# Two attention heads at a time: float32r scores over stacked rows, and forget sums added in masks by GpSimd

## The chip, the cores and the metric

The kernel runs on one core of one Trainium2 chip. The metric is device time in microseconds (us) of one execution. The engines of the core are PE (TensorE, matrix multiplication), ACT (ScalarE), DVE (VectorE), POOL (GpSimd) and SP (SyncE, which here only starts transfers). Each engine takes its own instructions in the order in which they are written, and waits on semaphores for the others.

## The reference, cut to what matters

Two layers of a decoder trunk are computed for 256 tokens of width 1024. Each layer is a half-step FFN, a mixer and a second half-step FFN. The change lies in the mixer. It has three groups of attention heads that read one projection `P = rms_norm(h) @ w_in`:

```python
# A: 4 heads that share one key and value head; each query keeps its top 64 keys
s = jnp.einsum('bqhd,bqkd->bhqk', qb, kg) * scale        # only selected keys
# B: 4 heads, causal; with 256 tokens one block, so plain causal attention
# C: 8 heads with a forget gate
log_f = log_sigmoid(cf + forget_bias)
c = cumsum(log_f, axis=1)                                # per head, over tokens
s = einsum(q, k) * scale + c[query] - c[key]             # then causal mask, softmax
o_c = (softmax(s) @ v) * sigmoid(cg)
h = h + concat(o_a, o_b, o_c) @ w_out
```

In C, queries and keys are RMS-normed per head of 64 values. All of it is float32.

## The kernel before, in words

Weights are streamed from HBM by SP in pieces of 1 MB into five buffers (`raw`). Each piece is split into a high part `wh` (ACT rounds it to float32r, line 117) and a low part `wl` (DVE subtracts, line 121). This splitting is called from many places as `W.pump()`. A float32 product is made as three float32r products (high x high, high x low, low x high; `mm3`).

The order of all work is the order in which the Python code emits it (`manual_schedule`): there is no scheduler. Tiles come from rotating pools, so an instruction can also wait until the last reader of a buffer is done. The PSUM tag `gu` has four banks, and so has `acc`.

A mixer is first a projection in eight chunks of four steps, 32 steps in all (`iq, ib, b, a, ck, cq, cv, cg`). Beside the matmuls of each step run the side jobs registered by `at_step(n, job)`: rotary embedding and norms on POOL, the indexer and its top-k on DVE, the whole of the four B heads, and at step 29 (`SUMS_STEP`) the cumulative forget sums `c` by a matmul with a triangle of ones.

Then comes the stage that the change rewrites, here called the A/C stage: the four A heads, the eight C heads, and between their pieces, as filler for PE, ten half-steps of the output projection (`out_halves`: six matmuls of 512 columns each, from `oT`, the transposed outputs of head pairs that are ready). It ends in `tail`, which does the rest of the output projection and begins the next norm. One head is five jobs:

- `scores(i)`: PE multiplies queries by keys into a `gu` bank; DVE adds a mask, takes the row maximum and writes to SBUF (line 1024, one instruction for each of two query blocks). A heads use float32r in two products (keys split into high and low). C heads use one float32 product of 66 rows (`cT`): 64 values, and two rows that carry `c` and ones, so that the product adds `c[query] - c[key]`. The mask of C is the plain causal one.
- `exps(i)`: two exponentials on ACT (lines 1031, 1032).
- `flip(i)`: three PE transposes into a bank, copied to SBUF by DVE (even heads) or ACT (odd heads) (line 1040).
- `values(i)`: PE multiplies with the values; DVE divides by the sum (lines 1054, 1060, 1063).
- `outT(j)`: for a pair of heads, two PE transposes, then ACT rounds to the high part (line 1078) and DVE subtracts for the low part (line 1079).

`c_T(j)` transposes queries and keys of a pair of C heads, eight PE transposes of 66 columns, one copy each on ACT and DVE (lines 1137, 1138). The loop runs over single heads: scores of head i, flip of head i-1, exponentials of head i, a `c_T`, an output half, an `outT`, values of head i-1.

Of the kernel before, what the change touches and what calls it, by code (L numbers as in the profile page):

```python
# [18 lines left out]
P = 128  # L19
S = 256  # L20
# [15 lines left out]
DOWN_LAG = 4  # L36
OUT_TAIL = 3
WARM = 6
BRIDGE = 3
# [102 lines left out]
def kernel(ctx: ExitStack, tc: tile.TileContext, x, ffn1_norm, ffn1_w_gate, ffn1_w_up, ffn1_w_down,  # L142
# [148 lines left out]
    identr = cp.tile([P, P], F32R, name="identr")  # L291
    cqa = [at.tile([P, 8, 66], F32, name=f"cqa{t}", tag=f"cqa{t}") for t in range(2)]
    cka = [at.tile([P, 8, 66], F32, name=f"cka{t}", tag=f"cka{t}") for t in range(2)]
    va = [at.tile([P, 13, 65], F32, name=f"va{t}", tag=f"va{t}") for t in range(2)]
    for t in range(2):
        G.memset(cqa[t][:, :, 65:66], 1.0)
        G.memset(cka[t][:, :, 64:65], 1.0)
        G.memset(va[t][:, :, 64:65], 1.0)
# [311 lines left out]
    def tail(acc, rhs, ks, factor, make_norm, late=None):  # L610

        nxt = make_norm()
        ws = dict(zip(ks, [W.take() for _ in ks]))

        def part(q, some):
            for k in some:
                tokens(acc[q], q, rhs[k], ws[k], False, k == ks[-1])

        ahead = [0] * 4
        if late:
            part(0, ks[:1])
            late[0]()
            part(0, ks[1:2])
            part(1, ks[:1])
            late[1]()
# [33 lines left out]
    def mixer(l, norm, nxt):  # L661
# [109 lines left out]
        def post_ib(ps):  # L771
# [182 lines left out]

        c_ss = at.tile([P, 2, 2, 8], F32, name="c_ss", tag="c_ss")

        def c_sums(i, dst, ps, when):
            sq = []
            for t in range(2):
                evac(dst[t][:, :, 0:64], heads(ps[t], 8), t)  # L960
                sq.append(squares(ps[t], t, 8))
# [7 lines left out]
        def post_ck(ps):  # L969
            c_sums(0, cka, ps, 21)  # L970

        def post_cq(ps):
            c_sums(1, cqa, ps, 25)
            for t in range(2):
                q = cqa[t][:, :, 0:64]
                G.tensor_tensor(q, q, gc[:, None, :].to_broadcast([P, 8, HD]), op=ALU.mult)

            def c_norm():
                rs = head_rs(c_ss.rearrange("p i t h -> p (i t h)"), 32, "c")
                for t in range(2):  # L980
                    for i, d in enumerate((cka, cqa)):
                        x = d[t][:, :, 0:64]
                        scale_heads(x, x, rs[:, 16 * i + 8 * t:16 * i + 8 * t + 8])

            at_step(25, c_norm)

        def post_cv(ps):
# [14 lines left out]
        def run_heads(hs, qk, tag, emit=None):  # L1002
            pj, pt, op = {}, {}, {}

            def scores(i):

                kind, h = hs[i]
                q, k = qk(kind, h)
                b = bank(tag)
                if kind == "C":  # L1010
                    mm(b[:, 0:P], q[:, 0:P], k[:, 0:P], True, True)
                    mm(b[:, P:3 * P], q[:, P:S], k[:, 0:S], False, True)
                else:
                    products(b[:, 0:P], q[:, 0:P], [c[:, 0:P] for c in k], True, True)
                    products(b[:, P:3 * P], q[:, P:S], [c[:, 0:S] for c in k], False, True)
                mask = st["amask"] if kind == "A" else causal
                s = tmp(3 * P)
                nm = sm.tile([P, 2], F32, name="nm", tag="nm")
                for t, c in enumerate((slice(0, P), slice(P, 3 * P))):
                    scale = -1.0  # L1020
                    if kind != "C":
                        col = (5 * t if kind == "A" else 4 * t) + h
                        scale = st["r" + kind.lower()][:, col:col + 1]
                    V.tensor_tensor_reduce(s[:, c], b[:, c], mask[:, c], scale, 3e38, op0=ALU.add, op1=ALU.min,
                                           accum_out=nm[:, t:t + 1])
# [39 lines left out]
            def outT(i):  # L1065
# [12 lines left out]
                A.copy(hh, b[:, :S])  # L1078
                V.tensor_tensor(hl, b[:, :S], hh.bitcast(F32), op=ALU.subtract)
                oT[k] = (hh, hl)  # L1080

            if emit is None:
                return scores, exps, flip, values, outT
            for fn, whens in ((scores, (-0.5, 0.5, 1.5, 2.5)), (exps, (0.25, 1.25, 3.25, 3.5)),
                              (flip, (2.6, 2.7, 4.6, 4.7)), (values, (4.3, 4.4, 5.3, 5.4)), (outT, (8.3, 8.4))):
                for i, when in enumerate(whens):
                    emit(when, lambda fn=fn, i=i: fn(i))

# [39 lines left out]

        c_both = xp.tile([P, 2, 8, S], F32, name="cT", tag="xhl")
        cT = [c_both[:, 0], c_both[:, 1]]  # L1130

        def c_T(hp_):
            for d, src in zip(cT, (cqa, cka)):
                b = bank("gu")
                for i in range(2):
                    for t in range(2):
                        T.transpose(b[:66, i * S + t * P:i * S + (t + 1) * P], src[t][:, 2 * hp_ + i, :], ident)  # L1137
                (A.copy if src is cqa else V.tensor_copy)(d[:66, 2 * hp_:2 * hp_ + 2],
                                                         b[:66].rearrange("p (a b) -> p a b", a=2))

        def qk_ac(kind, h):
            if kind == "A":
                return st["aqT"][:, h], [st["akT"][:, c, 0] for c in range(2)]
            return cT[0][:66, h], cT[1][:66, h]
# [3 lines left out]
        n = len(hs)  # L1148
        next(halves)
        for i in range(n + 1):  # L1150
            if i < n:
                scores(i)
            if i > 0:
                flip(i - 1)
            if i < n:
                exps(i)
            if i in (1, 3, 5, 7):
                c_T(i // 2)
            if i not in (3, 5, 7, n):
# [7 lines left out]
        return tail(acc, oT, OUT_ORDER[8 - OUT_TAIL:], 1.0, nxt,  # L1167
                    (lambda: values(n - 1), lambda: outT(n // 2 - 1)))

# [59 lines left out]
```

## Time and profile before

| what | value |
|---|---|
| median of 3 runs | 1038.47 us (1037.96 to 1039.38) |
| profiled execution | 1038.33 us |
| its span in the profile | 1036.6 us |
| busy share PE, DVE, ACT, POOL | 100%, 78%, 57%, 14% |
| granted TensorE clock | 1.0 of full speed |

The span is what the profile covers, from the first to the last instruction of the core; the time of the execution has some 1.7 us around it. Busy shares are averages over the whole program. A matmul's record includes its way through the array, so consecutive records overlap, and short waits of PE do not show in its busy share; starts of successive instructions, or the chain of work, tell what a matmul costs in a row. In the layer that is looked at, the projection ends and the A/C stage begins at 289.5 us of the span, and the next FFN begins at 336.8 us. The second layer runs the same code.

### The profile page before, as it was taken

What the parts mean: (1) busy time and instruction counts of PE and PEld (TensorE: products, weight loads), DVE (VectorE), ACT (ScalarE), POOL (GpSimd) and SP (SyncE); (2) the same over time, 40 slices, a digit from 0 to 9 for tenths busy, and PEclk for the clock granted to TensorE, in tenths of its full rate; (3) what the DMA queues carried; (4) which work ended last, traced back from release to release, by engine and by line L of the source; (5) the groups of instructions that cost most, each with busy time, mean ns of one, the idle gap of its engine ahead of it and who ended that gap; (6) DMA issues with size and microseconds to landing.
All of it is one profiled execution on the core that took longest, in us unless ns stands there. A gap on an engine that the chain in (4) does not pass through costs nothing.

```text
span 1036.6 us, 15084 instructions
## 1 busy us (share of the span) xinstructions
PE 1032.3 (100%) x5641; PEld 898.8 (87%) x5641; DVE 808.9 (78%) x1537; ACT 591.8 (57%) x1045; POOL 148.2 (14%) x177
## 2 busy tenths in 40 slices
PE   9999999999999999999999999999999999999998
PEld 8888888898888888888888888888988988888887
DVE  6978778789876877777788777787898768777776
ACT  6655555666854655555465555557676546555552
POOL 2003000167800000000000110002766000000000
PEclk9999999999999999999999999999999999999999
DMA  9674656555431364645645564664555224554631
GB/s 320 222 244 157 214 185 198 182 190 174 154 131 42 123 230 144 236 163 206 200 163 195 180 219 150 241 185 174 163 194 172 83 67 159 182 199 167 232 134 40
DMA packets 130808, 181.61 MB, mean 175 GB/s; under 512 B 7040, under 2 KB 104624, under 8 KB 130736
## 3 DMA queue, kind: packets, MB, share of 16 engines
q1 hardware_dynamic: 130704, 180.66, 51.5%
q8 instruction: 44, 0.72, 0.3%
q14 instruction: 28, 0.23, 0.1%
q10 hardware_dynamic: 32, 0.01, 0.0%
HBM read 179.60 MB, written 1.05 MB: 174 GB/s over the span
## 4 chain that ended last, share of the span: by engine, by line
PE 99%; DMA 1%; SPq 0%; DVE 0%; issue 0%
PE ps_gu L302 66%; PE ps_acc L302 30%; PE ps_acc L337 1%; PE ps_gu L1038 1%; PE ps_gu L1137 1%; DMA trunk<-in_x_dram 1%; PE ps_acc L739 0%; PE ps_acc L1038 0%; PE ps_gu L1071 0%; PE ps_acc L494 0%; SPq L91 0%; PE ps_acc L363 0%; PE ps_acc L1071 0%; SPq L190 0%; DVE trunk L376 0%
## 5 line engine op out<-in xcount | busy, mean ns | idle before, releaser
L121 DVE TENSOR_TENSOR wl<-raw,wh 128x1024 fp32r<-128x1024 f32 (+2 forms) x342 | 416.9, 1225 | 24.9 <-ACT wh L117 24.9
L117 ACT CAST wh<-raw 128x1024 fp32r<-128x1024 f32 (+2 forms) x341 | 343.0, 1036 | 5.7 <-PE ps_gu L302 4.9
L302 PE MATMUL ps_gu<-xhl,wh 128*128 128x512 f32 x1408 | 330.4, 390 | 0.0
L302 PEld LDWEIGHTS ps_gu<-xhl,wh 128*128 128x128 f32 x1408 | 262.7, 188 | 53.9 <-ACT wh L117 0.4
L302 PEld LDWEIGHTS ps_gu<-xhl,wl 128*128 128x128 f32 x1408 | 176.1, 191 | 4.2 <-issue 0.2
L302 PE MATMUL ps_gu<-xhl,wl 128*128 128x256 f32 x1408 | 179.1, 283 | 0.0
L302 PE MATMUL ps_gu<-wh,xhl 128*128 128x512 f32 (+2 forms) x512 | 157.2, 377 | 0.0
L441 DVE TENSOR_TENSOR tmp<-ps_gu,tmp 128x256 f32<-128x256 f32 x176 | 72.9, 422 | 107.7 <-ACT tmp L440 107.4
L302 PE MATMUL ps_acc<-wh,hh 128*128 128x512 f32 (+1 forms) x352 | 137.2, 390 | 0.0
L302 PE MATMUL ps_acc<-wl,hh 128*128 128x512 f32 (+1 forms) x352 | 137.0, 389 | 0.0
L302 PE MATMUL ps_acc<-wh,hl 128*128 128x512 f32 (+1 forms) x352 | 136.5, 388 | 0.0
L440 ACT COPY tmp<-ps_gu 128x256 f32<-128x256 f32 x176 | 63.5, 371 | 93.3 <-PE ps_gu L302 93.1
L302 PEld LDWEIGHTS ps_gu<-wh,xhl 128*128 128x128 f32 x512 | 94.8, 188 | 14.6
L455 ACT CAST hh<-tmp 128x256 fp32r<-128x256 f32 x80 | 32.6, 407 | 120.0 <-DVE tmp L452 120.0
L302 PE MATMUL ps_gu<-wl,xhl 128*128 128x512 f32 (+2 forms) x256 | 95.7, 374 | 0.0
L447 ACT ACTIVATE tmp<-tmp 128x256 f32<-128x256 f32 x88 | 36.9, 419 | 81.9 <-DVE tmp L445 81.6
L313 POOL TENSOR_TENSOR y_n<-msq,minus_half 128x2 f32<-128x2 f32 x6 | 6.8, 1141 | 529.7 <-DVE msq L312 529.7
L302 PEld LDWEIGHTS ps_acc<-wh,hl 128*128 128x128 f32 x352 | 66.1, 188 | 13.9
L302 PEld LDWEIGHTS ps_acc<-wh,hh 128*128 128x128 f32 x352 | 66.2, 188 | 12.6
L302 PEld LDWEIGHTS ps_acc<-wl,hh 128*128 128x128 f32 x352 | 66.3, 188 | 12.2
L302 PEld LDWEIGHTS ps_gu<-wl,xhl 128*128 128x128 f32 x256 | 48.2, 188 | 6.7
L326 ACT ACTIVATE xhl<-ps_acc,gT 128x256 fp32r<-128x256 f32 x48 | 19.1, 474 | 39.2 <-PE ps_acc L337 35.7
(221 smaller groups left out, 1010.8 us busy)
## 6 DMA issues: line engine op xcount, KB each, us to landing
raw<-in_ffn_w_down_dram SPq DMA_DIRECT2D x44, 1024.0 KB, 4.9
raw<-in_ffn_w_gate_dram SPq DMA_DIRECT2D x42, 1024.0 KB, 6.6
raw<-in_ffn_w_up_dram SPq DMA_DIRECT2D x42, 1024.0 KB, 7.5
raw<-in_w_in_dram SPq DMA_DIRECT2D x24, 1024.0 KB, 4.9
raw<-in_w_out_dram SPq DMA_DIRECT2D x8, 1024.0 KB, 4.9
raw<-in_w_in_dram SPq DMA_DIRECT2D x4, 768.0 KB, 4.9
raw<-in_w_in_dram SPq DMA_DIRECT2D x4, 656.0 KB, 4.0
raw<-in_ffn_w_gate_dram SPq DMA_DIRECT2D x3, 512.0 KB, 7.1
```

Of the source, the lines that this page charges most:

```text
L117: self.nc.scalar.copy(hv, src)
L121: (engine or self.nc.vector).tensor_tensor(lv, self.srcs[self.n_low], hv.bitcast(F32), op=ALU.subtract)
L302: T.matmul(o, l, r, start=start, stop=stop, skip_group_check=True)
L313: G.tensor_tensor(y, dst, minus_half[:, :n], op=ALU.pow)
L326: A.activation(self.h[:, m], src, AF.Copy, scale=gT[:, self.col + m:self.col + m + 1])
L337: T.transpose(ps[:, i, t * P:(t + 1) * P], trunk[:, t, (2 * mp + i) * P:(2 * mp + i + 1) * P], ident)
L440: A.copy(o, ps[:, 1])
L441: V.tensor_tensor(o, ps[:, 0], o, op=ALU.add)
L447: A.activation(th, t_, AF.Tanh, scale=0.5)
L455: (V.tensor_copy if late else A.copy)(hh, t_)
L1038: T.transpose(b[:, j * P:(j + 1) * P], pj[i][:, j * P:(j + 1) * P], ident)
L1137: T.transpose(b[:66, i * S + t * P:i * S + (t + 1) * P], src[t][:, 2 * hp_ + i, :], ident)
```

## The change

The A/C stage takes two heads at a time. The C scores no longer carry the forget sums in two extra rows. Queries and keys are now 128 stacked rows of float32r: the query's high part over its low part, and the key twice; the key's high and low parts are two products, as in A. The forget sums go into the mask: `c` is transposed by PE at step 30, its negative is written by ACT to a row buffer in DRAM and, at step 31, read back by one transfer that repeats it on all 128 partitions (8 heads x 256 values, 1 MB in SBUF). POOL then makes the masks for two heads at once, in place (`decay`), and prepares the stacked queries and keys (`c_parts`). The scaling of keys by their norm moves from `c_norm` to `c_parts`. In `c_T` both copies are now on ACT and a subtraction on DVE follows. `outT` gives back its DVE part, to be emitted between the two scores of the next pair. `HALVES` says how many output halves stand in each of the six iterations; two stand ahead of the loop.

```diff
+HALVES = (1, 2, 1, 1, 2, 1)
...
+dram = ctx.enter_context(tc.tile_pool(name="dram", bufs=1, space=bass.MemoryType.DRAM))
...
-                for t in range(2):
-                    c = b[:, 8 * t:8 * t + 8]
-                    A.copy(cqa[t][:, :, 64], c)
-                    A.activation(cka[t][:, :, 65], c, AF.Copy, scale=-1.0)
+                st["c"] = sm.tile([P, 2, 8], F32, name="c", tag="c", bufs=1)
+                A.copy(st["c"].rearrange("p t h -> p (t h)"), b[:, 0:16])
+
+            def turn_sums():
+                b = bank("acc")
+                for t in range(2):
+                    T.transpose(b[:8, t * P:(t + 1) * P], st["c"][:, t], ident)
+                n = tmp(S)[:8]
+                A.activation(n, b[:8, :S], AF.Copy, scale=-1.0)
+                st["row"] = dram.tile([8, S], F32, name="minus_c_row", tag="minus_c_row")
+                nc.scalar.dma_start(st["row"], n)
+
+            def load_sums():
+                d = st["row"]
+                st["minus_c"] = at.tile([P, 8, S], F32, name="minus_c", tag="kT")
+                nc.scalar.dma_start(st["minus_c"], bass.AP(tensor=d.tensor, offset=d.offset,
+                                                           ap=[[0, P], [S, 8], [1, S]]))
 
             at_step(SUMS_STEP, cumsum)
+            at_step(SUMS_STEP + 1, turn_sums)
+            at_step(SUMS_STEP + 2, load_sums)
...
+        def c_parts(j):
+            hs2 = slice(2 * j, 2 * j + 2)
+            q = tp.tile([P, 512], F32R, name="stacked", tag="tmp")
+            q4 = q.rearrange("p (t h s d) -> p t h s d", t=2, h=2, s=2)
+            A.copy(q4[:, :, :, 0], cq[:, :, hs2])
+            G.tensor_tensor(q4[:, :, :, 1], cq[:, :, hs2], q4[:, :, :, 0].bitcast(F32), op=ALU.subtract)
+            k = tmp(512)
+            k4 = k.rearrange("p (t h s d) -> p t h s d", t=2, h=2, s=2)
+            for t in range(2):
+                G.tensor_tensor(k4[:, t], ck[:, t, hs2, None, :].to_broadcast([P, 2, 2, HD]),
...
+        def decay(j):
+            m = st["minus_c"][:, 2 * j:2 * j + 2]
+            c = st["c"][:, :, 2 * j:2 * j + 2, None]
+            first = at.tile([P, 2, P], F32, name="first", tag="first", bufs=2)
+            tri2 = causal[:, None, 0:P].to_broadcast([P, 2, P])
+            G.tensor_tensor(first, m[:, :, 0:P], c[:, 0].to_broadcast([P, 2, P]), op=ALU.add)
+            G.tensor_tensor(first, first, tri2, op=ALU.add)
+            G.tensor_tensor(m, m, c[:, 1].to_broadcast([P, 2, S]), op=ALU.add)
+            G.tensor_tensor(m[:, :, P:S], m[:, :, P:S], tri2, op=ALU.add)
...
+            at_step(31, lambda: c_parts(0))
...
-                    mm(b[:, 0:P], q[:, 0:P], k[:, 0:P], True, True)
-                    mm(b[:, P:3 * P], q[:, P:S], k[:, 0:S], False, True)
+                    masks = decays.pop(h)
...
+            for i in range(2):
+                for t in range(2):
+                    mm(bq[:, i * S + t * P:i * S + (t + 1) * P], q[:, t, i], identr, i + t == 0, True)
+            for i in range(2):
+                for t in range(2):
+                    T.transpose(bk[:, i * S + t * P:i * S + (t + 1) * P], k[:, t, i], ident)
...
+            A.copy(d[:, 0], bq)
+            A.copy(d[:, 1], bk)
+            V.tensor_tensor(d[:, 2], bk, d[:, 1].bitcast(F32), op=ALU.subtract)
...
+        two(0, scores)
+        c_parts(1)
+        decay(0)
+        two(0, exps)
         next(halves)
...
+        next(halves)
+        for k in range(n):
+            last = k == n - 1
+            two(k, flip)
+            low = outT(k - 1) if k else None
+            if not last:
+                scores(2 * k + 2)
+            if low:
+                low()
+            if not last:
+                scores(2 * k + 3)
+                two(k + 1, exps)
+            if k < 4:
+                c_T(k)
+            if k < 3:
+                if k < 2:
+                    c_parts(k + 2)
+                decay(k + 1)
+            if not last:
+                two(k, values)
+            for _ in range(HALVES[k]):
                 next(halves)
-            if 0 < i < n:
-                if i > 2 and i % 2:
-                    outT((i - 3) // 2)
-                values(i - 1)
+            if last:
+                two(k, values)
```

More of the change, by code (lines that the diff above doesn't have):

```diff
@@ L622, in tail @@
         if late:
-            part(0, ks[:1])
-            late[0]()
-            part(0, ks[1:2])
+            part(0, ks[:2])
             part(1, ks[:1])
-            late[1]()
+            late()
             part(1, ks[1:2])
@@ L1009, in scores @@
                 b = bank(tag)
+                products(b[:, 0:P], q[:, 0:P], [c[:, 0:P] for c in k], True, True)
+                products(b[:, P:3 * P], q[:, P:S], [c[:, 0:S] for c in k], False, True)
                 if kind == "C":
[L1011 to L1016 removed]
+                    masks = decays.pop(h)
+                else:
+                    m = st["amask"] if kind == "A" else causal
+                    masks = m[:, 0:P], m[:, P:3 * P]
                 s = tmp(3 * P)
@@ L1078, in outT, with low @@
                 A.copy(hh, b[:, :S])
[L1079 removed]
                 oT[k] = (hh, hl)
+                def low():
+                    V.tensor_tensor(hl, b[:, :S], hh.bitcast(F32), op=ALU.subtract)
+                return low
             if emit is None:
@@ L1143, in qk_ac, with two @@
                 return st["aqT"][:, h], [st["akT"][:, c, 0] for c in range(2)]
-            return cT[0][:66, h], cT[1][:66, h]
+            d = cT[:, h // 2 % 2]
+            return d[:, 0, h % 2], [d[:, 1, h % 2], d[:, 2, h % 2]]
         hs = [("A", h) for h in range(4)] + [("C", h) for h in range(8)]
         scores, exps, flip, values, outT = run_heads(hs, qk_ac, "gu")
-        n = len(hs)
-        next(halves)
[L1150 to L1159, printed above, removed]
+        n = len(hs) // 2
+        def two(k, *fns):
+            for fn in fns:
+                fn(2 * k)
+                fn(2 * k + 1)
+        two(0, scores)
+        c_parts(1)
+        decay(0)
+        two(0, exps)
+        next(halves)
+        next(halves)
[19 more added lines that the diff above has]
+            for _ in range(HALVES[k]):
                 next(halves)
-            if 0 < i < n:
-                if i > 2 and i % 2:
-                    outT((i - 3) // 2)
-                values(i - 1)
+            if last:
+                two(k, values)
         for _ in halves:
             raise AssertionError
-        return tail(acc, oT, OUT_ORDER[8 - OUT_TAIL:], 1.0, nxt,
-                    (lambda: values(n - 1), lambda: outT(n // 2 - 1)))
+        return tail(acc, oT, OUT_ORDER[8 - OUT_TAIL:], 1.0, nxt, lambda: outT(n - 1)())
     def before_mixer(l):
```

44 lines of the change are left out of this document (22 added, 22 removed).

## The prediction

> **What bounds the kernel now.** I read the page first, then the A/C stage: its busy times, the chain of work and the instructions in order of time.
>
> ```profile
> span 1036.6 us, 15084 instructions
> ...
> PE 1032.3 (100%) x5641; PEld 898.8 (87%) x5641; DVE 808.9 (78%) x1537; ACT 591.8 (57%) x1045; POOL 148.2 (14%) x177
> ...
> PE 99%; DMA 1%; SPq 0%; DVE 0%; issue 0%
> ```
>
> PE is the chain from end to end. The stage that is rewritten, and in it the order of work on PE (start, duration, what):
>
> ```profile
> core 0: us, PE busy (x) PEld busy (x) DVE busy (x) ACT busy (x) POOL busy (x), PEclk, DMA share, GB/s
> 289.50:336.90 47.40, 47.40 (x306) 41.82 (x306) 32.77 (x112) 24.09 (x54) 0.00 (x0) 1.00 0.21 70
> ```
>
> ```profile
> 292.91 0.46 PE ps_gu L302 x4
> ...
> 310.44 1.32 PE ps_gu L302 x10
> 311.76 0.33 PE ps_gu L1038 x3
> 312.09 0.87 PE ps_gu L1137 x8
> 312.96 0.22 PE ps_gu L1071 x2
> ...
> 314.89 1.39 PE ps_acc L302 x6
> ```
>
> The granted clock is full (1.00) and PE goes from piece to piece without a gap; DVE is at 32.77 of 47.40 us (69%), ACT at 51%, POOL does nothing. So the stage is worth what its PE instructions cost, as long as the others keep up. A flip takes 0.33 us of PE, a c_T 0.87, an outT 0.22, an output half 1.39, values and scores of a C head together 1.32, scores of an A head alone 0.46. How the others follow, as instructions of one C head:
>
> ```profile
> 296.38 0.71 PE L302 MATMUL ps_gu<-akT,aqT 128*128 128x128 f32 x4
> 297.13 0.35 DVE L1024 CUSTOM_DVE_ANT_0 tmp<-ps_gu,amask,minus_a 128x128 f32<-128x128 f32 x1
> ...
> 310.27 0.78 PE L302 MATMUL ps_gu<-va,pT 128*128 128x65 f32 x6
> 310.89 0.87 PE L302 MATMUL ps_gu<-cT 66*128 66x128 f32 x4
> 311.09 0.17 DVE L1054 RECIPROCAL ri<-ps_gu 128x2 f32<-128x2 f32 x1 [0.47 <-PE ps_gu L302]
> ...
> 311.80 0.29 DVE L1024 CUSTOM_DVE_ANT_0 tmp<-ps_gu,causal 128x128 f32<-128x128 f32 x1
> ...
> 312.36 0.55 DVE L1040 COPY pT<-ps_gu 128x384 f32<-128x384 f32 x1
> 312.50 0.49 ACT L1032 ACTIVATE p<-tmp,nm 128x256 f32<-128x256 f32 x1
> 312.90 0.56 ACT L1138 COPY cT<-ps_gu 66x512 f32<-66x512 f32 x1
> 313.37 0.36 ACT L1078 CAST oh<-ps_gu 128x256 fp32r<-128x256 f32 x1
> 313.76 0.42 DVE L1079 TENSOR_TENSOR ol<-ps_gu,oh 128x256 fp32r<-128x256 f32 x1
> 314.10 0.16 DVE L1054 RECIPROCAL ri<-ps_gu 128x2 f32<-128x2 f32 x1
> ```
>
> From starts to starts: values cost PE 0.62 us, so C scores cost 1.32 - 0.62 = 0.70. DVE takes a score bank 0.75 us after its first matmul (A head), needs 0.56 for the mask of one C head, 0.34 for a low part, 0.71 to divide one C head (311.09 to 311.80), about 0.5 for a flip's copy. ACT needs 0.40 for the second exponential, 0.47 for a copy into `cT`.
>
> **The change, part by part** (us per layer; each counts twice).
>
> *PE, scores.* Eight C heads go from 0.70 to the price of A, which does the same matmuls: 0.46 alone, or some 0.51 behind other work: 1.5 to 1.9 saved, I take 1.7. Taking heads in pairs halves the returns from float32 to float32r; with no row for that here I bound it by 0 and 0.5 and take 0.3. Together -2.0. c_T keeps eight transposes, values, flips and outT their number, so nothing there.
>
> *PE, turn_sums.* Two transposes in the projection: 0.22 by the outT row, with a restart 0.25. It is on PE's path: +0.25.
>
> *The start of the stage.* ACT is now in front of a wait: the load of the sums waits, in ACT's order, until the row lies in DRAM, and behind it stand two weight roundings, the first stacked copy and the tanh of the gates; DVE's next weight subtraction and `hr` wait for those roundings, the tanh for `hr`, the first scores on DVE for the tanh.
>
> ```profile
> 287.01 1.05 ACT L117 CAST wh<-raw 128x1024 fp32r<-128x1024 f32 x1 [1.66 <-PE ps_gu L302]
> ...
> 288.62 1.22 DVE L121 TENSOR_TENSOR wl<-raw,wh 128x1024 fp32r<-128x1024 f32 x1
> ...
> 290.01 1.26 ACT L996 ACTIVATE sg<-ps_gu,hr 128x512 f32<-128x512 f32 x2 [1.95 <-DVE hr L993]
> ```
>
> ```profile
> raw<-in_w_out_dram SPq DMA_DIRECT2D x8, 1024.0 KB, 4.9
> ...
> out_dram<-trunk SPq DMA_DIRECT2D x3, 256.0 KB, 2.0
> ...
> tmp<-in_ffn_norm_dram ACTq DMA_DIRECT2D x1, 8.0 KB, 2.6
> ...
> fb<-in_forget_bias_dram SPq DMA_DIRECT2D x1, 8.0 KB, 5.1
> ```
>
> Step 30 ends two steps of 2.72 us (twice 12 matmuls at 0.227, a sixth of 1.39 less the switch) ahead of 289.5, at 284.1. Transposes 0.25 and the copy of the negative 0.4: issue at 284.9. The row lands after 2.0 to 2.6 us (a write, and the one small transfer on ACT's queue), at about 287.2; second issue, copy 0.4, rounding 1.05: 289.1; subtraction 1.22, `hr`: tanh at about 290.5 to 290.9 instead of 290.26 (290.01 and the 0.25). I take +0.5; below, 0, since ACT had 1.66 and 1.95 us of idle time; above, with 5.1 us to landing (a small load under load), +3. The 1 MB copy itself lands by about 294 (4.9 us for 1 MB, more beside a weight load) and POOL's first mask needs it, for C scores that come some 10 us into the stage: hidden, and with 10 us to landing still nearly so. SP's queue keeps its order.
>
> *POOL.* Per pair of heads: c_parts is one subtraction and two products of 128x256, decay three additions of 128x256 and one of 128x512.
>
> ```profile
> L686 POOL TENSOR_TENSOR bqr<-bqr,swapped 128x256 f32<-128x256 f32 x4 | 3.0, 738 | 0.3
> L685 POOL TENSOR_TENSOR bkr<-bkr,tab 128x256 f32<-128x256 f32 x4 | 5.0, 1260 | 0.3
> ...
> 276.19 1.04 POOL L691 TENSOR_TENSOR cka<-cka,y_c 128x512 f32<-128x512 f32 x1
> ...
> 277.25 4.05 DVE L121 TENSOR_TENSOR wl<-raw,wh 128x1024 fp32r<-128x1024 f32 x2
> ...
> 278.19 2.03 POOL L691 TENSOR_TENSOR cka<-cka,y_c 128x512 f32<-128x512 f32 x1
> ```
>
> At 0.74 and 1.04 a pair costs 6 x 0.74 + 1.04 = 5.5, at 1.26 and 2.03 9.6; an iteration lasts 5.4 to 6.8. The first rows are nearer (POOL then meets DVE only at weight subtractions), so the masks come in time and cost nothing themselves. But the last three rows show that POOL and a weight subtraction take turns: 1.04 becomes 2.03, and two subtractions of 1.22 take 4.05. The Trainium skill (GPSIMD Engine Reference, 8. Key points) says why: POOL shares its SBUF interfaces with VectorE and contends with VectorE instructions that have two SBUF inputs; the rows agree. It speaks against putting masks on POOL; by it the masks on DVE, which read PSUM and one SBUF tile, stay free of this.
>
> *The loop.* Here the gain is lost. I count from the start of one outT on PE, O(k). Scores follow 0.22 later, DVE reads them at 0.97; mask 0.56, low part 0.34 (now between the two), second mask 0.56: 2.43, its last row minimum 0.08 later. ACT's second exponential 0.40, then the two `cT` copies that are now both on ACT:
>
> ```profile
> L729 ACT CAST iqT<-ps_acc 128x512 fp32r<-128x512 f32 x8 | 4.3, 590 | 5.8 <-PE ps_acc L302 5.8
> L742 DVE TENSOR_TENSOR bkT<-ps_acc,bkT 128x512 fp32r<-128x512 f32 x4 | 2.5, 674 | 0.0
> ```
>
> That is 0.47, as in the order above, and 0.59 to the end of the second: 4.0. Only then can DVE subtract (0.67): 4.7. In DVE's order the divisions of two heads stand behind that subtraction, twice 0.71: 6.1. The next outT needs them. So O(k+1) is not before O(k) + 6.15 with C heads, 5.7 with A heads. PE's own work from O to O is two flips 0.66, O 0.22, scores 1.0, c_T 0.87, values 1.24 and 1.39 per half: 5.4 with one half, 6.8 with two. Iteration 1 has two halves: no wait. Iterations 2 and 3 (one half, c_T): 0.75 of waiting each, at O(2) and O(3). Iteration 0, whose chain begins behind the first exponentials, waits some 0.5 in flip and O(0). A weight subtraction (1.22) at the end of iteration 2 stands on DVE ahead of the even flip's copy, which ends at 6.1 + 1.2 + 0.5 = 7.8 instead of being ready; c_T wants that bank at 6.15 + 0.22 + 1.0 = 7.4, and the next mask starts at 7.8 instead of 7.1: +0.7 on the chain. Sum 2.7; three subtractions can meet POOL, each for 0 to 1.04, where only part is on the chain: +0.2. I take 2.9, between 0 (each step shorter than its row) and 4.
>
> Sum per layer: -2.0 + 0.25 + 0.5 + 2.9 = +1.65; two layers +3.3 on the profiled execution's 1038.33, which stands 0.14 below the median 1038.47: 1041.6 us.
>
> **The rivals.**
> *No waiting* (the other side). If the copies and the subtraction are through before PE needs them, that is, if the loop from O to O takes no more than 5.4, only -2.0 + 0.25 is left: -3.5, 1034.8. For it: DVE at 69% and ACT at 51% have room, and before, PE never waits. Against: the length is an order of dependent work, not a sum of busy time. It decides for faster once waiting and start cost less than 0.7 per layer (1.75 - 1.05).
> *Half of it.* Waiting of 1.5 and no loss at the start: -0.25 per layer, 1037.8; up to 2.8 it remains within 0.2% (2.1 us), about what a measurement can tell from no change.
> *The row lands late.* At 5.1 us instead of 2.6 the start slips by 2.5 per layer, of which PE's first halves hide nothing more: 1046.6. For it: the DMA engines are 83% busy here (the row below); against: the small transfer on ACT's own queue took 2.6.
>
> ```profile
> 286.00:289.50 3.50, 3.50 (x17) 2.92 (x16) 3.46 (x9) 1.05 (x1) 0.00 (x0) 1.00 0.83 267
> ```
>
> *Masks late.* With 1.26 and 2.03 throughout, POOL needs 9.6 a pair against 6: the fourth mask some 6 late, part of it in place of other waits: +2 per layer, 1045.6. Against: such lengths are seen only beside DVE work that is rare in this stage.
> *The change doesn't do what it says*: four float32r matmuls with four weight loads might cost no less than four float32 passes of 66 rows; the A row's 0.46 against 0.70 excludes it.
>
> **How the numbers follow.** Forecast (slower) 0.38; no waiting 0.26; half 0.22; late row 0.09; late masks 0.05. Slower by over 0.2%: 0.38 + 0.09 + 0.05 = 0.52; within: 0.22; faster: 0.26. The range reaches to the no-waiting case below and nearly to the late masks above, 1034.7 to 1045.5, and leaves out some 2 in 10; the forecast's own is 1040.5 to 1043.
>
> **What would show it.** In the chain, PE's share in the A/C stage falls for the first time, with ACT and DVE pieces (copies into `cT`, its subtraction, `o`) between; the stage is some 1.5 us longer while its C scores cost 0.5 us of PE; PE's starts have gaps ahead of outT in iterations 2 and 3; POOL is busy for some 20 us of the stage (four masks, three c_parts), and weight subtractions of over 2 us appear in it. The tanh starts later against the end of the projection. I am wrong if outT follows the flips at once (no waiting), or if waits end on POOL or on the DRAM row.

## The result and the profile after

The changed kernel takes 1041.9 us (median of 7 runs, 1041.62 to 1042.22) against 1038.06 us before (median of 7 runs as well, the first three of which gave the 1038.47 ahead of the prediction): a ratio of 1.0036, with a 95% interval of 1.0026 to 1.0046. That is 3.8 us slower, and clear of the noise.

From the page of the changed kernel: the span, the busy times and the chain of work that ended last.

```profile
span 1040.2 us, 15186 instructions
...
PE 1032.3 (99%) x5645; PEld 896.9 (86%) x5645; DVE 809.2 (78%) x1537; ACT 599.1 (58%) x1057; POOL 190.1 (18%) x225
...
PE 93%; POOL 3%; DVE 2%; ACT 1%; DMA 1%; issue 0%; SPq 0%; ACTq 0%; DVEq 0%
```

PE is busy for exactly as long as before (1032.3 us) and the span is 3.6 us longer; PE's share of the chain falls from 99% to 93%, and POOL, DVE and ACT stand in it. POOL's busy time rises from 148 to 190 us. (That POOL is named in the chain does not yet say that POOL costs time; the experiments below take it apart.)

The A/C stage of the first layer, busy time (instructions) of PE, weight loads, DVE, ACT and POOL, then clock, DMA share and GB/s:

```profile
core 0: us, PE busy (x) PEld busy (x) DVE busy (x) ACT busy (x) POOL busy (x), PEclk, DMA share, GB/s
289.50:338.60 49.10, 47.63 (x306) 41.21 (x306) 33.53 (x113) 27.39 (x61) 20.63 (x25) 1.00 0.25 87
```

The stage runs from 289.56 to 338.57, 49.0 us instead of 47.3, at full clock. In the second layer it takes 48.7 instead of 47.3 (802.60 to 849.93 before, 804.55 to 853.21 after). These 1.7 and 1.3 us are 3.0 of the 3.6 us; the rest is about what the four transposes of the two `turn_sums` were put at (0.25 per layer). POOL is busy for 20.6 us of the stage and PE no longer for all of it.

*What PE saves.* One iteration of the loop in which PE waits for nothing, of the changed kernel (start, duration, instruction; flips of two heads, outT, scores of two C heads, c_T, values of two heads, one output half, next flips):

```profile
307.09 0.82 PE L1083 MATMUL ps_gu<-ident,p 128*128 128x128 f32 x6
307.74 0.38 PE L1116 MATMUL ps_gu<-ident,o 128*128 128x128 f32 x2
307.88 1.17 PE L302 MATMUL ps_gu<-cT 128*128 128x128 f32 x8
308.88 0.56 PE L302 MATMUL ps_gu<-identr,stacked 128*128 128x128 f32 x4
...
309.92 1.46 PE L302 MATMUL ps_gu<-va,pT 128*128 128x65 f32 x12
311.19 0.48 PE L302 MATMUL ps_acc<-wh,oh 128*128 128x512 f32 x1
...
312.66 0.82 PE L1083 MATMUL ps_gu<-ident,p 128*128 128x128 f32 x6
```

The same work before, two heads one after the other (values, scores, flip, c_T, outT, then values, scores and flip of the second head, the half, the next values):

```profile
304.43 0.78 PE L302 MATMUL ps_gu<-va,pT 128*128 128x65 f32 x6
305.04 0.87 PE L302 MATMUL ps_gu<-cT 66*128 66x128 f32 x4
305.75 0.49 PE L1038 MATMUL ps_gu<-ident,p 128*128 128x128 f32 x3
306.08 0.60 PE L1137 MATMUL ps_gu<-ident,cqa 128*66 128x128 f32 x4
...
306.95 0.38 PE L1071 MATMUL ps_gu<-ident,o 128*128 128x128 f32 x2
307.17 0.83 PE L302 MATMUL ps_gu<-va,pT 128*128 128x65 f32 x6
...
308.80 0.48 PE L302 MATMUL ps_acc<-wh,oh 128*128 128x512 f32 x1
...
310.27 0.78 PE L302 MATMUL ps_gu<-va,pT 128*128 128x65 f32 x6
```

From starts to starts, before: values, scores and flips of the two heads 0.61 + 0.71 + 0.33 and 1.63, c_T 0.87, outT 0.22, the half 1.47; together 5.84. After: flips 0.65, outT 0.14, scores 1.00, c_T 1.04, values 1.27, the half 1.47; together 5.57. Scores cost 0.50 per head instead of 0.71, as forecast. But c_T costs 0.17 more. It has eight instructions on PE as before, but not the same ones: the four for the keys (L1189) are transposes of 128 columns instead of 66 and take 0.49 instead of 0.43, and the four for the queries (L302, `identr,stacked`) are now float32r products with an identity and take 0.55 instead of 0.44. Its weight loads, before and after (the last columns are busy us, mean ns, idle time before):

```profile
L1137 PEld LDWEIGHTS ps_gu<-ident,cqa 128*66 128x66 f32 x32 | 3.5, 112 | 0.0
```

```profile
L302 PEld LDWEIGHTS ps_gu<-identr,stacked 128*128 128x128 f32 x32 | 4.2, 190 | 1.9 <-POOL minus_c L997 1.2 <-POOL first L994 0.7
...
L1189 PEld LDWEIGHTS ps_gu<-ident,tmp 128*128 128x128 f32 x32 | 3.4, 141 | 0.3
```

The load that took 112 ns for 66 columns takes 190 and 141 ns for 128, which is the likely reason; it was not tested by itself. So this pair of C heads saves 0.27 us, not the quarter of 2.0.

One iteration is not the stage, so the second layer's stage was also added up by kind of work, from each start to the next, for the kernel before (47.33 us) and for "the same, scalings moved" of the table below (45.94 us, of which PE waits 0.2): C scores 5.70 and 4.31 (1.00 for a pair, 1.30 for the one that waits), A scores 2.01 and 1.93, c_T 3.41 and 3.89, values 7.59 and 7.58, and flips, outT and output halves together 27.82 and 27.45 (only together, since what stands ahead of an instruction counts too: in the changed kernel a half behind values takes 1.47, one behind another half 1.37). So c_T costs 0.5 more per layer, and without waits PE saves about 1.5 us per layer, not 2.0.

*What waits.* By iteration, first flip to first flip, and in brackets what the same iteration's PE work takes where nothing waits: from the start of the stage to the first flip 4.12 (3.65); iteration 0 6.40 (5.17); iteration 1 7.01 (6.97); iteration 2 5.57; iteration 3 6.44 (5.59); iteration 4 6.51 (5.9). The bracketed times come from kernels below in which PE does not wait at that place; the last is from their second layer, where iteration 4 takes 5.89 to 5.92. The waits sum to 0.47 + 1.23 + 0.04 + 0.85 + 0.6 = 3.2 us. Half of the last 0.6 stands ahead of outT; the other half stands in the values of iteration 4, in the first layer alone (1.50 us against 1.26 in the second), and its cause is open. With PE's 1.5 saved and the 0.25 of `turn_sums` that makes +1.95 us per layer; measured is half of 3.84, +1.9.

### The profile page after: what moved, and what is told of

The parts are those of the page before. It is cut to its first block, busy times and chain, and to the rows that moved or that the text cites. A ratio compares the mean times of both kernels' runs of the same rounds, so it can differ in the third digit from the quotient of the medians.

```text
span 1040.2 us, 15186 instructions
## 1 busy us (share of the span) xinstructions
PE 1032.3 (99%) x5645; PEld 896.9 (86%) x5645; DVE 809.2 (78%) x1537; ACT 599.1 (58%) x1057; POOL 190.1 (18%) x225
## 4 chain that ended last, share of the span: by engine, by line
PE 93%; POOL 3%; DVE 2%; ACT 1%; DMA 1%; issue 0%; SPq 0%; ACTq 0%; DVEq 0%
PE ps_gu L302 63%; PE ps_acc L302 28%; DVE wl L122 1%; PE ps_acc L337 1%; POOL tmp L983 1%; POOL first L994 1%; DMA trunk<-in_x_dram 1%; POOL minus_c L997 0%; POOL minus_c L996 0%; PE ps_gu L1083 0%; POOL stacked L979 0%; POOL first L995 0%; PE ps_acc L737 0%; PE ps_acc L1083 0%; ACT sg L1041 0%
## 5 line engine op out<-in xcount | busy, mean ns | idle before, releaser
L302 PE MATMUL ps_gu<-xhl,wh 128*128 128x512 f32 x1408 | 330.3, 390 | 0.3 <-DVE xhl L329 0.3
L302 PEld LDWEIGHTS ps_gu<-xhl,wh 128*128 128x128 f32 x1408 | 262.7, 188 | 54.3 <-issue 0.4
L302 PEld LDWEIGHTS ps_gu<-xhl,wl 128*128 128x128 f32 x1408 | 176.0, 191 | 4.3 <-issue 0.2
L302 PE MATMUL ps_gu<-xhl,wl 128*128 128x256 f32 x1408 | 179.1, 283 | 0.1
L302 PE MATMUL ps_gu<-wh,xhl 128*128 128x512 f32 (+2 forms) x512 | 157.7, 378 | 0.0
L302 PE MATMUL ps_acc<-wh,hh 128*128 128x512 f32 (+1 forms) x352 | 137.2, 390 | 0.0
L302 PE MATMUL ps_acc<-wl,hh 128*128 128x512 f32 (+1 forms) x352 | 137.0, 389 | 0.0
L302 PE MATMUL ps_acc<-wh,hl 128*128 128x512 f32 (+1 forms) x352 | 136.5, 388 | 0.0
L302 PEld LDWEIGHTS ps_gu<-wh,xhl 128*128 128x128 f32 x512 | 94.7, 188 | 14.5
L302 PE MATMUL ps_gu<-wl,xhl 128*128 128x512 f32 (+2 forms) x256 | 95.6, 374 | 0.0
L302 PEld LDWEIGHTS ps_acc<-wh,hl 128*128 128x128 f32 x352 | 66.1, 188 | 13.9
L302 PEld LDWEIGHTS ps_acc<-wh,hh 128*128 128x128 f32 x352 | 66.3, 188 | 12.6
L302 PEld LDWEIGHTS ps_acc<-wl,hh 128*128 128x128 f32 x352 | 66.2, 188 | 12.2
L302 PEld LDWEIGHTS ps_gu<-wl,xhl 128*128 128x128 f32 x256 | 48.2, 188 | 6.6
```

The costliest lines, as they stand in the source:

```text
L302: T.matmul(o, l, r, start=start, stop=stop, skip_group_check=True)
```

## Experiments

In each, the theory of the prediction (the stage is now set by the order of dependent work on ACT and DVE, and not by PE or POOL) stands against rivals. The table gives the median and the stage of the first layer in the profiled execution, from the first scores of A (before: from the output half that opens the stage) to the first matmul of the FFN:

| kernel | median us | stage us | against before (95%) |
|---|---|---|---|
| before | 1038.0 to 1038.3 | 47.30 | |
| changed | 1041.90 | 49.01 | 1.0026 to 1.0046 |
| parts of the first pair early | 1041.24 | 48.57 | 1.0018 to 1.0041 |
| low part behind the divisions | 1039.33 | 47.73 | 1.0002 to 1.0019 |
| without POOL's masks | 1041.58 | 48.65 | 1.0020 to 1.0045 |
| float32 scores | 1044.34 | 50.18 | 1.0044 to 1.0072 |
| sums not from the row | 1041.86 | 49.01 | 1.0024 to 1.0051 |
| start of the stage | 1040.00 | 47.89 | 1.0009 to 1.0027 |
| start, low part and parts | 1037.62 | 46.87 | 0.9987 to 1.0004 |
| start, low part, half moved | 1037.28 | 46.64 | 0.9983 to 1.0001 |
| the same, scalings moved | 1036.54 | 46.27 | 0.9976 to 0.9994 |
| the same, parts early | 1036.55 | 46.32 | 0.9978 to 0.9995 |

Twice the difference of an edited kernel's stage to that of the changed one is the difference of their medians within 0.4 us throughout (with the scalings moved: 2 x 2.74 = 5.5 against 5.36), so the first layer's stage may be read for the whole.

### The start of the stage: the row in DRAM, or turns of POOL and DVE

The tanh, behind which the first masks and flips stand, starts at 291.20 instead of 290.01. Instructions of the changed kernel in order of time:

```profile
284.69 0.51 ACTq L883 DMA_DIRECT2D minus_c_row<-tmp  x1
...
285.99 0.35 ACTq L888 DMA_DIRECT2D minus_c<-minus_c_row  x1
...
286.87 1.29 POOL L979 TENSOR_TENSOR stacked<-cq,stacked 128x256 fp32r<-128x256 f32 x1 [7.73 <-ACT stacked L978]
...
287.47 0.77 DVE L857 TENSOR_SCALAR amask<-score 128x128 f32<-128x128 f32 x1
...
288.12 1.23 POOL L983 TENSOR_TENSOR tmp<-ck,y_c 128x256 f32<-128x256 f32 x2
288.16 1.34 DVE L859 SCALAR_TENSOR_TENSOR amask<-score,cst 128x128 f32<-128x128 f32 x2
...
289.56 1.08 PE L302 MATMUL ps_gu<-akT,aqT 128*128 128x128 f32 x8
...
291.20 1.27 ACT L1041 ACTIVATE sg<-ps_gu,hr 128x512 f32<-128x512 f32 x2 [2.50 <-DVE hr L1038]
...
293.68 0.33 PE L1083 MATMUL ps_gu<-ident,p 128*128 128x128 f32 x1 [0.31 <-ACT p L1076]
```

Before, the same two kinds of mask operations on DVE:

```profile
287.69 0.22 DVE L859 TENSOR_SCALAR amask<-score 128x128 f32<-128x128 f32 x1
287.83 0.49 DVE L861 SCALAR_TENSOR_TENSOR amask<-score,cst 128x128 f32<-128x128 f32 x2
```

The row is not late: the load that waits for it is issued 1.30 us after the write's issue. DVE reaches A's mask even earlier than before (287.47 against 287.69). But there it meets POOL, which makes the parts of the first C heads: 0.22 becomes 0.77 and 0.49 becomes 1.34. That is 1.4 of loss, and the weight subtraction, `hr` and the tanh stand behind it.

Two experiments tell the causes apart. One takes the wait for the row away:

```diff
-                d = st["row"]
+                d = w_out
```

> Edit: the 1 MB copy of the sums is loaded from the output weights, which lie in DRAM from the start, so it no longer waits for the row (wrong numbers stand in for the forget sums; the row is still written). Theory (turns): ACT's wait for the row costs nothing on the path, 1041.9, within 0.5 us. Rival (row, as the prediction had it: half a us per layer at the start of the stage): about 1 us less, 1040.9.

1041.86 us, no change, and the stage takes 49.01 us as in the changed kernel. There is a wait for the row, since without it the load is issued 0.58 us after the write and not 1.30, but it costs nothing on the path; the prediction's cause falls. The other moves POOL:

```diff
-            at_step(31, lambda: c_parts(0))
+            at_step(28, lambda: c_parts(0))
```

> Edit: the parts of the first two C heads are made at step 28 of the projection instead of step 31, so that POOL is through with them before DVE makes the mask of A. Theory (turns): the changed kernel's tanh starts 1.2 us late because POOL's c_parts(0) and DVE's three mask operations take turns (0.77 and 1.34 us instead of 0.22 and 0.49); then these go back to 0.22 and 0.49, the tanh starts about 1 us earlier, and the time falls by 1 to 2 us from 1041.9, to about 1040.2. Rival (row): the start is late because ACT's queue waits for the row of sums in DRAM; that wait stays where it is, so no change, 1041.9.

1041.24 us (1040.97 to 1041.86): 0.7 less, short of the 1 to 2 that were expected. The instructions of this kernel:

```profile
288.36 0.22 DVE L857 TENSOR_SCALAR amask<-score 128x128 f32<-128x128 f32 x1
...
288.49 0.49 DVE L859 SCALAR_TENSOR_TENSOR amask<-score,cst 128x128 f32<-128x128 f32 x2
...
290.69 1.27 ACT L1041 ACTIVATE sg<-ps_gu,hr 128x512 f32<-128x512 f32 x2 [2.35 <-DVE hr L1038]
...
293.18 0.33 PE L1083 MATMUL ps_gu<-ident,p 128*128 128x128 f32 x1
```

The mask operations are back at 0.22 and 0.49, as the theory of turns has it, and the tanh starts at 290.69. That only 0.5 us of 1.2 came back has its reason earlier, on ACT:

```profile
279.12 0.41 ACT L978 CAST stacked<-cq 128x256 fp32r<-128x256 f32 x1 [1.00 <-POOL cq L689]
...
281.93 0.76 DVE L1127 TENSOR_TENSOR ol<-ps_acc,oh 128x256 fp32r<-128x256 f32 x2 [1.77 <-ACT oh L1123]
```

The first stacked copy of the queries now waits 1.00 us for POOL's scaling of `cq`, and in ACT's order a weight rounding and the copies `va` and `oh` stand behind it; DVE's low part `ol` waits 1.77 us for `oh` (0.83 in the changed kernel), and DVE comes to the mask 0.9 us later (288.36 against 287.47). One wait was removed and another set in its place.

The rows of the changed kernel also say which DVE instructions take turns with POOL: not only an operation with two SBUF inputs (L859), but also one with a single SBUF input and an SBUF output (L857). C masks that read PSUM do not: 0.28 and 0.42 us for one head, with POOL busy or, in the kernel without POOL's masks, idle. The Trainium skill (SBUF — State Buffer, Who interferes with whom) names these cases: the port pair that DVE shares with POOL is held for a whole instruction, and DVE needs it with two SBUF inputs or in a 2-port mode, and not otherwise. The rows agree; that L857 runs in such a mode is not seen in them, only that it takes turns.

Next, everything at the start that stands in front of the first masks without need was moved: `hr` to step 28, DVE's two scalings of the gates from `post_cg` to the end of iteration 0.

```diff
+            def half_r():
+                st["hr"] = sm.tile([P, 2], F32, name="hr", tag="hr")
+                V.tensor_scalar(st["hr"], norm.r, 0.5, None, op0=ALU.mult)
+            at_step(28, half_r)
...
-            for t in range(2):
-                V.tensor_scalar(sg[:, t], sg[:, t], 0.5, 0.5, op0=ALU.mult, op1=ALU.add)
...
+            if k == 0:
+                for t in range(2):
+                    V.tensor_scalar(st["sg"][:, t], st["sg"][:, t], 0.5, 0.5, op0=ALU.mult, op1=ALU.add)
             for _ in range(HALVES[k]):
```

> Edit: hr is made at step 28, ahead of the weight subtraction that it stood behind, and DVE's two scalings of the gates (0.43 us each) go from the front of the first masks to the end of iteration 0. Theory (the start of the stage costs 0.4 us ahead of the first flip and 1.2 us inside iteration 0, as the trace of the changed kernel shows, because tanh, scaling and masks follow one another): 1.2 to 1.6 us per layer come back, 1038.7 to 1039.5. Rival (the first iteration is bound by something else, POOL's parts or the two weight subtractions): 0.5 us per layer or less, 1041 or more.

1040.00 us, between the two. The start was as the theory has it: the first flip comes 3.65 us after the first scores (4.12) and iteration 0 takes 5.17 (6.40), which is 1.7 us. The mask operations still take 0.77 and 1.33 us in this kernel: at the start of the stage the turns cost time only as long as `hr` and the tanh stand behind them. But iteration 1 now takes 7.51 instead of 7.01: the scalings stand in front of a flip's copy there. Half a microsecond was given back one iteration later.

### The loop: DVE's divisions behind ACT's copies

In iterations 2 and 3 of the changed kernel (the last column in brackets is the idle time before and what ended it):

```profile
311.80 0.69 DVE L1193 TENSOR_TENSOR cT<-ps_gu,cT 128x512 fp32r<-128x512 f32 x1 [1.54 <-ACT cT L1192]
...
313.58 1.22 DVE L122 TENSOR_TENSOR wl<-raw,wh 128x1024 fp32r<-128x1024 f32 x1
...
313.62 0.43 PE L1116 MATMUL ps_gu<-ident,o 128*128 128x128 f32 x2
...
314.71 0.55 DVE L1085 COPY pT<-ps_gu 128x384 f32<-128x384 f32 x1
...
315.41 0.63 PE L302 MATMUL ps_gu<-identr,stacked 128*128 128x128 f32 x4 [0.43 <-POOL minus_c L997]
...
320.06 0.43 PE L1116 MATMUL ps_gu<-ident,o 128*128 128x128 f32 x2
```

DVE's subtraction of the keys' low part waits 1.54 us for ACT's second copy into `cT`; the divisions, a weight subtraction and a flip's copy (`pT`) stand behind it in DVE's order. The flips of iterations 3 and 4 start at 312.66 and 319.10 and outT 0.96 us later instead of 0.65: 0.31 of waiting each. The queries' part of c_T at 315.41 waits some 0.6 us for a PSUM bank. The experiment puts the subtraction behind the divisions:

```diff
-            V.tensor_tensor(d[:, 2], bk, d[:, 1].bitcast(F32), op=ALU.subtract)
+            def key_low():
+                V.tensor_tensor(d[:, 2], bk, d[:, 1].bitcast(F32), op=ALU.subtract)
+            return key_low
...
-            if k < 4:
-                c_T(k)
+            key_low = c_T(k) if k < 4 else None
...
                 two(k, values)
+            if key_low:
+                key_low()
```

> Edit: in the loop, DVE's subtraction that makes the low part of the keys stands behind the divisions of the two heads instead of in front of them, so that these no longer wait for ACT's two copies into cT. Theory (order of dependent work): the waits ahead of outT in iterations 2 and 3 (0.3 and 0.4 us) and part of that in the first iterations go: 0.5 to 1.2 us per layer, 1039.5 to 1040.9. Rival (PE is paced by its own work or by POOL's masks): the wait moves to the next step, no change within 0.5 us of 1041.9.

1039.33 us, 2.6 less, a little more than expected. Its rows for flips and outT of iteration 3 and the flips of iteration 4:

```profile
313.02 0.82 PE L1083 MATMUL ps_gu<-ident,p 128*128 128x128 f32 x6
313.67 0.38 PE L1116 MATMUL ps_gu<-ident,o 128*128 128x128 f32 x2
...
318.61 0.81 PE L1083 MATMUL ps_gu<-ident,p 128*128 128x128 f32 x6
```

outT follows the flips after 0.65, and iteration 3 takes 5.59 us instead of 6.44, iteration 4 6.15 instead of 6.51: 1.2 us per layer, all that the two waits and the late bank had cost. One instruction's place in DVE's order was two thirds of the whole loss.

### POOL's masks

```diff
-            G.tensor_tensor(first, m[:, :, 0:P], c[:, 0].to_broadcast([P, 2, P]), op=ALU.add)
...
-                decays[2 * j + i] = first[:, i], m[:, i]
+                decays[2 * j + i] = causal[:, 0:P], causal[:, P:3 * P]
```

> Edit: POOL's four additions per pair of C heads are left out and the C scores take the plain causal mask (the forget sums are left out of the result; the row is still written and loaded). Theory (POOL in time): POOL's masks cost only where they take turns with DVE's weight subtractions and in one 0.56 us wait for the first mask of a pair: 0.3 to 0.8 us per layer, 1040.3 to 1041.3. Rival (masks late): if the loop is paced by POOL, 2 us per layer or more come back, below 1038.

1041.58 us, 0.3 less, which is no more than the runs of one kernel spread, under the 0.6 to 1.6 that were expected, and far from the rival. The masks come in time. The row that answers to the wait at 315.41 above, which the profile puts down to POOL's mask:

```profile
315.33 0.63 PE L302 MATMUL ps_gu<-identr,stacked 128*128 128x128 f32 x4 [0.43 <-DVE pT L1077]
```

The same 0.43 us with no mask on POOL at all, now put down to `pT`, the flip's copy on DVE that frees the bank. The name behind a wait is that of the last event, not always that of the cause, so the share of the chain that bears the masks' name is no price of the masks. (What POOL's parts cost at the start of the stage is another matter: 0.7 us by the run with the parts early.)

### What the scores are worth

```diff
+                if kind == "C":
+                    mm(b[:, 0:P], q[:, 0:P], k[0][:, 0:P], True, True)
+                    mm(b[:, P:3 * P], q[:, P:S], k[0][:, 0:S], False, True)
...
-        cT = xp.tile([P, 2, 4, 2, S], F32R, name="cT", tag="xhl")
+        cT = xp.tile([P, 2, 4, 2, S], F32, name="cT", tag="xhl")
```

> Edit: the C scores go back to one float32 product (of stacked queries and unsplit keys, 128 rows), the low part of the keys is still made but not read; all else as changed. Theory (the scores' term as forecast): PE gets back 0.21 us per C head and 0.3 for the switches, 2.0 us per layer; about half of it lies in waits that are there anyway: 1044 to 1046. Rival (the saving was smaller than forecast, about 1 us per layer): 1042.5 to 1044.

1044.34 us: 2.4 more, 1.2 per layer. It lies at the foot of the first band, which had 2.0 per layer with half of that hidden; but the rows show that next to nothing was hidden, and that the price was smaller. Scores of two heads, then c_T, then values:

```profile
308.08 1.49 PE L302 MATMUL ps_gu<-cT 128*128 128x128 f32 x8
309.22 0.75 PE L302 MATMUL ps_gu<-identr,stacked 128*128 128x128 f32 x4
...
310.26 1.45 PE L302 MATMUL ps_gu<-va,pT 128*128 128x65 f32 x12
```

Float32 scores of two heads over 128 rows take 1.14 us, 0.57 per head, where one head over 66 rows took 0.71 before. Float32r brings them to 0.50, and an iteration without waits from 5.78 (307.21 to 312.99) to 5.57: 0.21 per pair (0.08 of it outT's, which takes 0.22 again), 0.8 per layer; the rest of the 1.2 is longer waits (iteration 3 takes 6.96 instead of 6.44). So two thirds of what a head's scores save against before (0.14 of 0.21) come with the stacking and the pairs, and one third with float32r. Whether it is the rows or the pairs was not separated.

### Putting the order right

The three edits together:

> Edit: the start of the stage as in the run before, the low part of the keys behind the divisions, the parts of the first pair at step 28: three edits at once. Theory (waits and PE's saving add up): PE saves about 1 us per layer against the kernel before and nearly all waits go: 1041.9 - 2.6 - 3 - 0.5 = 1035.8, faster than before (1038.1). Rival (the edits remove the same wait twice): 1038 to 1039.3.

1037.62 us: the sum of the three gains (0.66 + 2.57 + 1.90 = 5.1) would have given 1036.8; 4.3 came, between the theory's 1035.8 and the rival's 1038. Iteration 3 still takes 6.35 instead of 5.59: its weight subtraction, now at 310.42, takes 2.10 us beside POOL instead of 1.22, and the flip's copy behind it frees c_T's bank late. Instead of the early parts, one output half was then moved into iteration 0:

```diff
-HALVES = (1, 2, 1, 1, 2, 1)
+HALVES = (2, 1, 1, 1, 2, 1)
```

> Edit: start of the stage and low part as in the run before, the parts of the first pair at step 31 as changed, and one output half moved from iteration 1 to iteration 0 (2, 1, 1, 1, 2, 1). Theory (iteration 0 has waits that a half can fill, iteration 1 is without): 0 to 0.7 us per layer below the same without the move, about 1035.5 to 1037. Rival (iteration 1 then waits in the place of iteration 0): 1037 to 1039.

1037.28 us, in the rival's band, though the 0.3 below the run before is within the noise. The rival's sign is there too: iteration 3 is free (5.59), but iteration 1 waits. DVE's order there, and PE's wait in the second head's scores:

```profile
298.18 1.50 DVE L1244 TENSOR_SCALAR sg<-sg 128x512 f32<-128x512 f32 x2
...
299.60 1.63 DVE L122 TENSOR_TENSOR wl<-raw,wh 128x1024 fp32r<-128x1024 f32 x1
...
301.75 0.44 PE L302 MATMUL ps_gu<-cT 128*128 128x128 f32 x2 [0.47 <-DVE pT L1087]
```

The two scalings take 1.50 us beside POOL, not 2 x 0.43, the weight subtraction 1.63, and PE waits 0.47 us for the copy behind them. So the scalings go to a place where DVE idles, ahead of iteration 0's divisions:

```diff
             key_low = c_T(k) if k < 4 else None
+            if k == 0:
+                for t in range(2):
+                    V.tensor_scalar(st["sg"][:, t], st["sg"][:, t], 0.5, 0.5, op0=ALU.mult, op1=ALU.add)
...
                 two(k, values)
...
-            if k == 0:
-                for t in range(2):
-                    V.tensor_scalar(st["sg"][:, t], st["sg"][:, t], 0.5, 0.5, op0=ALU.mult, op1=ALU.add)
```

> Edit: as the run with the halves moved (2, 1, 1, 1, 2, 1), with DVE's two scalings of the gates ahead of iteration 0's divisions, where DVE idles, instead of at its end. Theory (in that run iteration 1 waits 0.47 us for a flip's copy on DVE, which stands behind the scalings, 1.50 us beside POOL, and a weight subtraction of 1.63): 0.3 to 0.5 us per layer below it, 1036.3 to 1036.7. Rival (the weight subtraction alone makes the copy late): no change, 1037.3.

1036.54 us, as the theory had it: 5.4 us below the changed kernel and 1.5 below the one before, with a ratio of 0.9985 (0.9976 to 0.9994). The chain of its page, and the flips of iterations 1 to 3:

```profile
PE 99%; DMA 1%; SPq 0%; DVE 0%; issue 0%
```

```profile
300.30 0.81 PE L1085 MATMUL ps_gu<-ident,p 128*128 128x128 f32 x6
...
305.85 0.82 PE L1085 MATMUL ps_gu<-ident,p 128*128 128x128 f32 x6
...
311.44 0.82 PE L1085 MATMUL ps_gu<-ident,p 128*128 128x128 f32 x6
```

PE is the whole chain again, and iterations 1 and 2 take 5.55 and 5.59 us. Last, the first pair's parts at step 28 in this kernel:

> Edit: as the run with the scalings moved, and the parts of the first pair at step 28. Theory (POOL off DVE's mask operations, worth 0.3 us per layer where the start has no waits left, since two output halves stand between the scores and the first flip): 1036 to 1036.7. Rival (POOL then meets a weight subtraction of the projection, and the start has cover anyway): no change against the run before, or 0.5 us more.

1036.55 us, no change: the time lies in the theory's band too, but the 0.3 us per layer that the theory had for the early parts did not come. So the rival holds, the start has cover by then.

## Why the prediction was right, and where it was not

The time was forecast at 1041.6 and is 1041.9, and the reason held: PE's saving is outweighed by waits of PE on an order of dependent work, which the profile of before could not show since there was no wait in it. But the terms were off, and part of the agreement is that their errors cancel.

- **Scores, -2.0 per layer: measured -1.5.** The price of the scores was right (0.71 to 0.50 per head, 1.7 in all). The 0.3 for fewer returns to float32r agrees with the 0.37 that flips, outT and output halves save together, though no run takes those returns by themselves. The step that failed is "c_T keeps eight transposes, values, flips and outT their number, so nothing there": the number is the same, but four of the eight are float32r products now, all load 128 columns instead of 66, and c_T costs 0.5 more per layer.
- **turn_sums, +0.25:** agrees with what is left of the difference of the spans outside the two stages (0.6 us for two).
- **Start, +0.5: measured 0.5 up to the first flip, by another cause, so the size agrees by luck.** The forecast had ACT waiting for the row in DRAM; the load behind the row was issued 1.3 us after the write, and the row costs nothing. DVE's mask operations took turns with POOL, which the prediction had said to happen "only at weight subtractions". Of the 1.40 us lost there, 0.85 are L859's, which has two SBUF inputs and was left out of the count, and 0.55 are L857's, which has one.
- **Loop, +2.9: measured 2.7.** The sum is near, its parts are not. Iteration 0 was taken at 0.5 and is 1.23: the masks of the second head follow the late tanh and the scalings, and moving these gave all of it back. O(2) and O(3) were taken at 0.75 each and are 0.31 each: the order was right, but the chain from one outT to the next (307.74 to 313.62) took 5.88 and not 6.15, and PE's own work took 5.57 and not 5.4, which is c_T's 0.17 again. The even flip's copy behind a weight subtraction in iteration 3 was taken at 0.7 and is 0.6. The 0.24 in the values of iteration 4 were not in the forecast. POOL's 0.2 is not distinguishable from the 0.15 per layer that the masks cost in all.
- **POOL in time:** right, 0.61 to 0.74 for 128x256 and 1.04 for 128x512, some 20 us of the stage, and 0.3 us in all when the masks are left out. The weight subtractions of over 2 us that were to show it did not come in the changed kernel: the longest in the first layer's stage takes 1.61 us.
- **Rivals.** "No waiting" could not have given 1034.8: with PE's measured saving its end is about 1038.06 + 2 x (0.25 - 1.5) = 1035.6; the kernel with the fewest waits (0.5 us in the first layer, 0.2 in the second) measures 1036.54. "Half of it" needed waits of 1.5 per layer in the loop and none at the start; they were 2.7 and 0.5. "Row late" and "masks late" are excluded by the two runs that remove them (1041.86 and 1041.58).

What stays open is the cause of the 0.14 us per head that float32 scores save over 128 rows and in pairs, that of the 0.24 us in the values of iteration 4, and whether the wider loads alone make c_T dearer.

## What to carry to other kernels

Where one engine is the whole chain, price a change on it from start to start over a whole iteration, with every instruction whose shape changes, and then write down the order of the dependent work on the other engines for the new order of emission: the place of one DVE subtraction in front of two divisions cost 2.6 us here, about all that the change saved on PE net of `turn_sums` (2 x (1.5 - 0.25) = 2.5). An engine that had been idle is not free to use: here POOL took turns with DVE at masks that have nothing to do with POOL's own work. And before a wait is blamed on the engine that the profile names, leave that engine's work out once.

## What was not expected of the hardware

- A DVE operation with one SBUF input and an SBUF output takes turns with POOL too: 0.22 became 0.77 us (128x128), and two scalings of 0.43 took 1.50.
- A row of 8 KB written to DRAM on ACT's queue let the load that waits for it issue 1.3 us after the write's own issue (0.58 where the load does not wait for it).
- Float32 scores over 128 rows for two heads in a row cost 0.57 us per head, against 0.71 for single heads over 66 rows; float32r with a second product costs 0.50.
